# Attention on one core: GpSimd casts tied to VectorE's PSUM reads, and eight score groups on VectorE

## The chip, the core and the metric

The kernel runs on one core of a Trainium2 chip. The time is the device time of one execution in microseconds, the median of ten runs: 122.35 us (121.79 to 123.35). A core has a matrix engine (TensorE, PE in the profile, with PEld for its weight loads), VectorE (DVE), ScalarE (ACT), GpSimd (POOL) and SyncE (SP), whose queue issues nearly all transfers here. SBUF is the on-chip memory; PSUM is the small memory that TensorE writes its results to. Each engine works through its own instructions in order; semaphores hold an instruction until what it needs is done.

## The reference

```python
# q, k, v: (8 batches, 8 heads, 512 positions, 64) float32
scale = 1.0 / np.sqrt(64)
scores = np.einsum('bhqd,bhkd->bhqk', q, k) * scale
scores = scores - scores.max(axis=-1, keepdims=True)
attn = np.exp(scores)
attn = attn / attn.sum(axis=-1, keepdims=True)
out = np.einsum('bhqk,bhkd->bhqd', attn, v)
```

The kernel leaves out the subtraction of the maximum, which cancels in the quotient, and gets the sum from a column of ones that stands beside v.

## The kernel before, in words

The 64 heads are 32 pairs, g = 0 to 31. For each pair the kernel loads q, k and v (256 KB each, float32), casts them to float16, transposes q and k on TensorE, copies the transposed tile from PSUM to SBUF, and then works through eight blocks of scores: 128 keys by 512 queries for each of four key chunks c and two heads h. Two blocks make a group, numbered m; pair g has groups 4g to 4g + 3, and the last two blocks of all stand alone, so there are 129 groups. Scores of a group fill one tile `st` of 128 x 1024 float32 in PSUM (two banks); there are three such tiles. So the scores of group m can start only when whatever reads group m - 3 is done with it.

Most groups get their exponential on ScalarE (L391). Some get it on VectorE instead, in six instructions: `raise_` (L406) reads the scores from PSUM and writes z to SBUF, which frees the PSUM tile. Five `pass_` instructions follow, from SBUF to SBUF: the first takes the mantissa bits (m, L420), and four make a quartic polynomial of it (y, y, y and the result `pd`, L430). The float16 result is the upper half of each 32-bit word. In the names of this text, pass 86.3 is pass 3 (counted from 0) of group 86, and raise 102 the raise of group 102.

TensorE then multiplies the exponentials by v (`values`, L464): a unit is 128 queries of one head, four matmuls of 65 columns. Seven units share a PSUM bank; `normalise` (a reciprocal, L442, and a multiplication, L443) empties the bank on VectorE, and each head that is complete is stored from there (L451). "Norm 168" is the one that begins with unit 168. Two PSUM banks are shared between these outputs and the transposes, which `copy` (L364) empties on VectorE. "Copy 26" is that of pair 26. The last head of all (L479) is summed over the key chunks as they come, and is normalised and stored apart (L491 to L499).

The order is not left to a scheduler: the block at the end of the kernel is written with manual order, and `Plan` makes the list of steps. It holds a clock for TensorE, ScalarE and VectorE with assumed durations (`COPY`, `NORM`, `RAISE`, `PASSES`), and picks the next step of each engine from what would be ready. `for_dve` decides whether a group goes to VectorE: only when no pass of another group is waiting (`AHEAD` 0), at most `MOST` groups, none in the last `LAST_PAIRS` pairs. `LATE_NORM` and `LATE_COPY` say how late a copy or norm may be made by starting a pass before it, `MARGIN` stretches the passes, `SLACK` is added before values may use what VectorE made. On the chip only the resulting order counts; the assumed times are not used.

GpSimd does the casts (L340 for q and k, L332 for v) in the order of `feed(g)`, which comes at the first group of pair g: it issues the loads of pair g + 5, then the casts of q and k of pair g + 3, then of v of pair g + 2. A cast waits for its load and for a free buffer, and for nothing else.

Of the kernel before, what the change touches and what calls it, by code (L numbers as in the profile page):

```python
# [9 lines left out]
FP16 = mybir.dt.float16  # L10
# [3 lines left out]
AluOp = mybir.AluOpType  # L14


class Plan:
# [17 lines left out]

    COPY, NORM, RAISE = (615, 700), (307, 390), (1145, 1225)
    NORM_COLUMN, PASS_DONE = 67, 80
    PASSES = (690, 1335, 1335, 1335, 1335)
    FIRST_EXP = 5260
    STEP = 5  # L40
    FIRST_UNIT = 4

    LATE_NORM, LATE_COPY, HURRY, SOON, BACKLOG = 600, 800, 1000, 220, 1000
    LAST_PAIRS, AHEAD, MARGIN, SLACK, MOST = 5, 0, 1.1, 0, 7

    def __init__(self, groups, pairs, first):
        self.groups, self.pairs = groups, pairs
# [151 lines left out]
    def step_dve(self, t):  # L199
        now = [x for x in self.ready if x[0] <= t]  # L200
        if now:
# [11 lines left out]
            else:  # L213
                self.dve = t + self.RAISE[0]
                self.read[what[0]] = t + self.RAISE[1] + self.TO_PE
                self.passes += [(what[0], s) for s in range(len(self.PASSES))]
        elif self.passes:
            m, s = self.passes[0]
            end = t + int(self.MARGIN * self.PASSES[s])
            late = {"copy": self.LATE_COPY, "norm": self.LATE_NORM, "raise": self.LATE_NORM}  # L220
            if all(x[0] > end - late[x[1]] for x in self.ready):
                self.passes.pop(0)
                self.note(t, "pass", m, s)
                self.dve = end
                if s == len(self.PASSES) - 1:
                    self.exps[m] = end + self.PASS_DONE + self.TO_PE + self.SLACK
# [15 lines left out]
def kernel(  # L242
# [30 lines left out]
    qpool = ctx.enter_context(tc.tile_pool(name="qk16", bufs=3))  # L273
# [17 lines left out]
    raw = {}  # L291
    qkp = {}
    tqk = {}
    tps = {}
# [34 lines left out]
    def cast_v(g):  # L329
        if g >= NP:  # L330
            return
        nc.gpsimd.tensor_copy(out=vps[g % NV][:, :, :, 0:D], in_=raw[g]["v"][:, :, :, :])  # L332

    def cast_qk(g):
        if g >= NP:
            return
        t = qpool.tile([P, 2, NI, P], FP16, tag="qkp", name=f"qkp_{g}")
        for n, name in ((1, "k"), (0, "q")):
            eng = nc.vector if (g, name) == (1, "q") else nc.gpsimd
            eng.tensor_copy(  # L340
                out=t[:, n].rearrange("p i (h d) -> p h i d", h=2),
                in_=raw[g][name][:, :, :, :],
            )
        qkp[g] = t

    def feed(g):
        load(g + 5, "kqv")
        cast_qk(g + 3)
        cast_v(g + 2)

    def transposes(g, n, bank):
        if n == 0:
            tqk[g] = tpool.tile([P, 2, S], FP16, tag="tqk", name=f"tqk_{g}")
            tps[g] = ps_x.tile([P, 2, NI, P], FP16, tag=f"x{bank}", name=f"tp_{g}")
        n = 1 - n
        for i in range(NI):
            nc.tensor.transpose(tps[g][:, n, i, :], qkp[g][:, n, i, :], ident)  # L357

    def copy(g):
        if g == 1:  # L360
            for n in (1, 0):
                nc.vector.tensor_copy(out=tqk[g][:, n], in_=tps[g][:, n].rearrange("p i c -> p (i c)"))  # L362
            return
        nc.vector.tensor_copy(  # L364
            out=tqk[g][:, :, :], in_=tps.pop(g).rearrange("p n i c -> p n (i c)")
        )

    def scores(m, on_dve):
# [32 lines left out]
    QUARTIC = (0.013185735294320473 * 2.0**-78, 0.1618325836988675 * 2.0**-26, -0.6832878102805021, 0.5087543266551143 * 2.0**26)  # L401

    def raise_(m):
        r = raised[m]
        r["z"] = wpool.tile([P, 2, S], U32, tag="z", name=f"z_{m}")
        nc.vector.tensor_scalar(  # L406
            out=r["z"][:, :, :],
            in0=r["st"][:, :, :],
            scalar1=scale * 1.4426950408889634 * 2.0**26,
            scalar2=15 * 2.0**26,  # L410
            op0=AluOp.mult,
            op1=AluOp.add,
        )

    def pass_(m, s):
        r = raised[m]
        if s == 0:
            r["m"] = wpool.tile([P, 2, S], U32, tag="m", name=f"m_{m}")
            r["y"] = wpool.tile([P, 2, S], FP32, tag="y", name=f"y_{m}")
            nc.vector.tensor_scalar(  # L420
                out=r["m"][:, :, :],
                in0=r["z"][:, :, :],
                scalar1=0x03FFFFFF,
                scalar2=0x04000000,
                op0=AluOp.bitwise_and,
                op1=AluOp.bitwise_or,
            )
            return
        n = s - 1
        nc.vector.scalar_tensor_tensor(  # L430
            out=r["bits"][:, :, :] if n == 3 else r["y"][:, :, :],
            in0=r["m"][:, :, :] if n == 0 else r["y"][:, :, :],
            scalar=QUARTIC[n],
            in1=r["z"][:, :, :] if n == 3 else r["m"][:, :, :],
            op0=AluOp.mult if n == 0 else AluOp.add,
            op1=AluOp.add if n == 3 else AluOp.mult,
        )

    def normalise(u, n):
        o, x = os[u // 7], u % 7  # L440
        rc = opool.tile([P, 7, 1], FP32, tag="rc", name=f"rc_{u}")
        nc.vector.reciprocal(out=rc[:, 0:n], in_=o[:, x : x + n, D : D + 1])  # L442
        nc.vector.tensor_tensor(  # L443
            out=ring[:, u % NU : u % NU + n, :],
            in0=o[:, x : x + n, 0:D],
            in1=rc[:, 0:n].broadcast_to([P, n, D]),
            op=AluOp.mult,
        )
        while heads and heads[0][2] + NI <= u + n:
            g, h, u0 = heads.pop(0)  # L450
            nc.sync.dma_start(  # L451
                out=source(out, g)[:, h], in_=ring[:, u0 % NU : u0 % NU + NI, :]
            )

    def values(g, h, y, u, bank):

        if (g, h) == (LAST, 1):
            return last_values(y, bank)
        if y == 0:
            heads.append((g, h, u))  # L460
        if u // 7 not in os:
            os[u // 7] = ps_x.tile([P, 7, D + 1], FP32, tag=f"x{bank}", name=f"o_{u // 7}")
        for c in range(NI):
            nc.tensor.matmul(  # L464
                os[u // 7][:, u % 7, :],
                blocks[(g, c, h)][:, y * P : (y + 1) * P],
                vps[g % NV][:, h, c, :],
                start=(c == 0),
                stop=(c == NI - 1),
            )  # L470
# [132 lines left out]
    with tc.manual_schedule():  # L603
        first_loads()
        load(1, "kq")
        load(0, "v")
        for g in range(2, 5):
            load(g, "kq")
            load(g - 1, "v")
        load(4, "v")  # L610
        make_identity(nc, ident)
        for n in range(NV):
            nc.vector.memset(vps[n][:, :, :, D : D + 1], 1.0)
        first_pair()
        cast_qk(1)
        cast_v(0)
        cast_qk(2)
        cast_v(1)
        feed(0)
        do = {  # L620
            "transposes": transposes,
            "scores": scores,
            "values": values,
            "feed": feed,
            "raise": raise_,
            "copy": lambda g, b: copy(g),
            "pass": pass_,
            "norm": lambda u, n, b: normalise(u, n),
        }
        for what, *args in Plan(groups, NP, 3).run():  # L630
            do[what](*args)
# [30 lines left out]
```

## Time and profile before

| What | Value |
|---|---|
| Median of ten runs | 122.35 us |
| The profiled execution | 122.26 us |
| Its span, first to last instruction | 120.5 us |
| ScalarE busy | 113.5 us, 94% |
| TensorE busy | 104.3 us, 87% |
| VectorE busy | 99.5 us, 83% |
| GpSimd busy | 77.9 us, 65% |
| Moved by DMA | 33.82 MB |
| Granted TensorE clock, mean | 0.992 |

In the lists of groups, a row gives line, engine, operation, what is written from what, shapes and count, then after the bar the busy time in us, the mean of one in ns, and the idle time of that engine just before such instructions. In a timeline, a row gives the start and duration in us, engine, line, operation, tiles and count, and in brackets the idle time before it and what ended that. Records of ScalarE and VectorE can overlap their successor's, so the step from one start to the next is shorter than the duration.

### The profile page before, as it was taken

Reading aid. Unit: us, or ns where it says so; the run is one execution under the profiler, and the core shown is the slowest. Engines: PE = TensorE matmul, PEld = TensorE weight load, DVE = VectorE, ACT = ScalarE, POOL = GpSimd, SP = SyncE. Lnnn points to the kernel's source line nnn. Section 1 sums busy time; section 2 is a strip of 40 time slices with the busy share of each in tenths; the row PEclk is TensorE's granted clock in tenths of the full one; section 3 lists DMA queues with packets and bytes.
Section 4 is the critical chain, followed back from the end, with each engine's and each line's share of the span. In section 5 each row is a group of like instructions: output and inputs, shape, how many; then the busy total and the mean of one; then the engine's idle time right before and its main releaser. Section 6 shows DMA issues by size and latency. Waiting matters only on the chain.

```text
span 120.5 us, 3950 instructions
## 1 busy us (share of the span) xinstructions
PE 104.3 (87%) x1557; PEld 66.2 (55%) x1557; DVE 99.5 (83%) x171; ACT 113.5 (94%) x126; POOL 77.9 (65%) x101
## 2 busy tenths in 40 slices
PE   7977988899897989889987998999988889989970
PEld 2543645466463766457653656656754556667550
DVE  1457997999999998988999988898979999986261
ACT  4599999999999999999999999999999999999970
POOL 2469999995887476945886985775869499100000
PEclk9999999999999999999999999999999999999996
DMA  3999999999999999999999899999999981414253
GB/s 101 297 372 382 384 377 385 381 349 298 348 354 304 272 294 347 312 316 277 305 340 300 271 273 320 339 277 348 336 327 313 331 278 50 132 48 133 93 169 95
DMA packets 35603, 33.82 MB, mean 281 GB/s; under 512 B 2688, under 2 KB 35584, under 8 KB 35584
## 3 DMA queue, kind: packets, MB, share of 16 engines
q1 hardware_dynamic: 35152, 33.24, 85.4%
q10 hardware_dynamic: 432, 0.33, 0.8%
q8 instruction: 12, 0.20, 0.7%
q14 instruction: 7, 0.06, 0.1%
HBM read 25.17 MB, written 8.39 MB: 278 GB/s over the span
## 4 chain that ended last, share of the span: by engine, by line
ACT 50%; PE 27%; DVE 10%; issue 7%; DMA 2%; SPq 1%; ACTq 0%
ACT pt L391 50%; PE st L386 11%; PE o L464 8%; PE tp L357 3%; PE st_0a L512 3%; DVE ring L443 3%; DMA k<-in_k_dram 2%; DVE z L406 2%; DVE tqk L364 1%; DVE pd L430 1%; DVE rc L442 1%; PE st L555 1%; SPq L451 1%; DVE tqk L362 1%; DVE m L420 0%
## 5 line engine op out<-in xcount | busy, mean ns | idle before, releaser
L391 ACT ACTIVATE pt<-st 128x1024 f16<-128x1024 f32 (+1 forms) x119 | 108.5, 1291 | 0.1
L386 PE MATMUL st<-tqk 64*128 64x512 f16 x248 | 46.1, 382 | 10.8 <-ACT pt L391 7.4
L464 PEld LDWEIGHTS <-pt 128*128 128x128 f16 x952 | 35.6, 98 | 11.2 <-issue 9.1
L464 PE MATMUL o<-vp,pt 128*128 128x65 f16 x952 | 41.6, 194 | 0.2
L340 POOL CAST qkp<-k 128x512 f16<-128x512 f32 x31 | 28.6, 922 | 19.1 <-DMA k<-in_k_dram 6.9
L332 POOL CAST vp<-v 128x512 f16<-128x512 f32 x32 | 28.6, 894 | 1.2 <-DMA v<-in_v_dram 1.0
L386 PEld LDWEIGHTS <-tqk 64*128 64x128 f16 x248 | 13.5, 93 | 27.7 <-issue 18.8
L443 DVE TENSOR_TENSOR ring<-o,rc 128x448 f32<-128x448 f32 (+2 forms) x37 | 22.7, 612 | 1.3
L340 POOL CAST qkp<-q 128x512 f16<-128x512 f32 x30 | 22.3, 745 | 1.6 <-DMA q<-in_q_dram 1.5
L364 DVE COPY tqk<-tp 128x1024 f16<-128x1024 f16 x30 | 20.5, 686 | 2.6 <-PE tp L357 2.1
L357 PE MATMUL tp<-ident,qkp 128*128 128x128 f16 x248 | 19.2, 220 | 0.4 <-DVE ring L443 0.4
L430 DVE SCALAR_TENSOR_TENSOR y<-y,m 128x1024 f32<-128x1024 f32 x14 | 18.7, 1336 | 0.0
L357 PEld LDWEIGHTS <-qkp 128*128 128x128 f16 x248 | 14.1, 98 | 7.4 <-issue 4.3
L442 DVE RECIPROCAL rc<-o 128x7 f32<-128x7 f32 (+2 forms) x37 | 7.4, 199 | 7.2 <-PE o L464 7.0
L430 DVE SCALAR_TENSOR_TENSOR pd<-y,z 128x1024 uint32<-128x1024 f32 x7 | 9.6, 1373 | 0.0
L406 DVE TENSOR_SCALAR z<-st 128x1024 uint32<-128x1024 f32 x7 | 8.5, 1219 | 1.2 <-PE st L386 1.2
L430 DVE SCALAR_TENSOR_TENSOR y<-m 128x1024 f32<-128x1024 uint32 x7 | 8.9, 1278 | 0.0
L464 PE MATMUL o<-vp,pd 128*128 128x65 f16 x56 | 8.2, 194 | 0.0
L464 PEld LDWEIGHTS <-pd 128*128 128x128 f16 x56 | 5.5, 98 | 0.0
L420 DVE TENSOR_SCALAR m<-z 128x1024 uint32<-128x1024 uint32 x7 | 5.2, 737 | 0.0
L512 PE MATMUL st_0a<-const-bfloat16-1.0 128*128 128x512 bf16 (+1 forms) x11 | 3.5, 484 | 0.8 <-PEq L646 0.8
L512 PEld LDWEIGHTS <-const-bfloat16-1.0 128*128 128x128 bf16 x15 | 1.7, 131 | 2.4 <-issue 2.4
(44 smaller groups left out, 19.7 us busy)
## 6 DMA issues: line engine op xcount, KB each, us to landing
out_dram<-ring SPq DMA_DIRECT2D x63, 128.0 KB, 3.8
k<-in_k_dram SPq DMA_DIRECT2D x31, 256.0 KB, 4.7
q<-in_q_dram SPq DMA_DIRECT2D x31, 256.0 KB, 4.9
v<-in_v_dram SPq DMA_DIRECT2D x27, 256.0 KB, 5.1
v<-in_v_dram SPq DMA_DIRECT2D x10, 128.0 KB, 4.9
k<-in_k_dram ACTq DMA_DIRECT2D x2, 128.0 KB, 2.8
q<-in_q_dram SPq DMA_DIRECT2D x2, 128.0 KB, 2.6
out_dram<-obl SPq DMA_DIRECT2D x1, 64.0 KB, 1.6
```

What stands on the lines that cost most here:

```text
L332: nc.gpsimd.tensor_copy(out=vps[g % NV][:, :, :, 0:D], in_=raw[g]["v"][:, :, :, :])
L340: eng.tensor_copy(out=t[:, n].rearrange("p i (h d) -> p h i d", h=2), in_=raw[g][name][:, :, :, :],)
L357: nc.tensor.transpose(tps[g][:, n, i, :], qkp[g][:, n, i, :], ident)
L364: nc.vector.tensor_copy(out=tqk[g][:, :, :], in_=tps.pop(g).rearrange("p n i c -> p n (i c)"))
L386: nc.tensor.matmul(st[:, x, :], kc, qc, start=True, stop=True)
L391: nc.scalar.activation(out=pt[:, 0:size, :], in_=st[:, 0:size, :], func=EXP, scale=scale)
L406: nc.vector.tensor_scalar(out=r["z"][:, :, :], in0=r["st"][:, :, :], scalar1=scale * 1.4426950408889634 * 2.0**26, scalar2=15 * 2.0**26, o ...
L430: nc.vector.scalar_tensor_tensor(out=r["bits"][:, :, :] if n == 3 else r["y"][:, :, :], in0=r["m"][:, :, :] if n == 0 else r["y"][:, :, :] ...
L442: nc.vector.reciprocal(out=rc[:, 0:n], in_=o[:, x : x + n, D : D + 1])
L443: nc.vector.tensor_tensor(out=ring[:, u % NU : u % NU + n, :], in0=o[:, x : x + n, 0:D], in1=rc[:, 0:n].broadcast_to([P, n, D]), op=AluOp. ...
L464: nc.tensor.matmul(os[u // 7][:, u % 7, :], blocks[(g, c, h)][:, y * P : (y + 1) * P], vps[g % NV][:, h, c, :], start=(c == 0), stop=(c == ...
L512: nc.tensor.matmul(dst[:, 0:n], ones[:, 0:P], ones[:, 0:n], start=True, stop=True)
```

## The change

There are two parts. First, `feed` no longer issues casts but puts them in a list (`hold`). `copy`, `raise_` and `normalise`, the three steps that read PSUM on VectorE, each take one cast from the list (a raise two) and issue it with a dependency on the VectorE instruction recorded last, that is the one before the PSUM read. If the list has more than six entries, the oldest are issued without such a dependency; `needed` does the same when transposes or values come up whose cast is still in the list. In the order that results, 78 casts are released by VectorE's steps, 10 leave because the list is too long, and none leave by `needed`.

Second, the constants of `Plan` change, and with them the order. Eight groups go to VectorE instead of seven: 6, 17, 32, 46, 60, 72, 86 and 102, where it was 6, 22, 37, 53, 69, 86 and 102. The places of copies, norms, passes and values move with that.

```diff
-    PASSES = (690, 1335, 1335, 1335, 1335)
+    PASSES = (660, 1200, 1200, 1200, 1200)
...
-    LATE_NORM, LATE_COPY, HURRY, SOON, BACKLOG = 600, 800, 1000, 220, 1000
-    LAST_PAIRS, AHEAD, MARGIN, SLACK, MOST = 5, 0, 1.1, 0, 7
+    LATE_NORM, LATE_COPY, HURRY, SOON, BACKLOG = 1300, 1400, 1100, 220, 1000
+    LAST_PAIRS, AHEAD, MARGIN, SLACK, MOST = 3, 0, 1.05, 400, 8
...
+    def dve(ins):
+        latest[:] = [ins]
+        return ins
+
+    def release(n=1):
+        for g, name in held[:n]:
+            ins = cast(g, name)
+            if latest:
[...]
+        del held[:n]
+
+    def hold(g, names):
+        held.extend((g, name) for name in names if g < NP)
+        while len(held) > 6:
+            cast(*held.pop(0))
+
+    def needed(g, names):
+        while any((g, name) in held for name in names):
+            cast(*held.pop(0))
 
     def feed(g):
         load(g + 5, "kqv")
-        cast_qk(g + 3)
-        cast_v(g + 2)
+        hold(g + 3, "kq")
+        hold(g + 2, "v")
 
     def transposes(g, n, bank):
         if n == 0:
+            needed(g, "kq")
...
     def copy(g):
...
-        nc.vector.tensor_copy(
-            out=tqk[g][:, :, :], in_=tps.pop(g).rearrange("p n i c -> p n (i c)")
+        release()
+        dve(
+            nc.vector.tensor_copy(
+                out=tqk[g][:, :, :], in_=tps.pop(g).rearrange("p n i c -> p n (i c)")
+            )
         )
...
     def raise_(m):
+        release(2)
...
     def normalise(u, n):
         o, x = os[u // 7], u % 7
         rc = opool.tile([P, 7, 1], FP32, tag="rc", name=f"rc_{u}")
+        release()
...
         if y == 0:
+            needed(g, "v")
             heads.append((g, h, u))
```

`cast(g, name)` is `cast_qk` and `cast_v` in one, for one tensor at a time, and `dve(...)` stands around the copies, raises, passes and the multiplication of `normalise`.

More of the change, by code (lines that the diff above doesn't have):

```diff
@@ L327, in load, with cast @@
             nc.sync.dma_start(out=t[:, :, :, :], in_=source(src, g))
-    def cast_v(g):
+    def cast(g, name):
         if g >= NP:
             return
[L332 to L342, printed above, removed]
-            )
-        qkp[g] = t
+        if name == "v":
+            return nc.gpsimd.tensor_copy(
+                out=vps[g % NV][:, :, :, 0:D], in_=raw[g]["v"][:, :, :, :]
+            )
+        if g not in qkp:
+            qkp[g] = qpool.tile([P, 2, NI, P], FP16, tag="qkp", name=f"qkp_{g}")
+        eng = nc.vector if (g, name) == (1, "q") else nc.gpsimd
+        return eng.tensor_copy(
+            out=qkp[g][:, "qk".index(name)].rearrange("p i (h d) -> p h i d", h=2),
+            in_=raw[g][name][:, :, :, :],
+        )
+    held = []
+    latest = []
+    SYNC = mybir.DependencyInfo(mybir.DependencyClass.Sync, mybir.DependencyReason.DATA)
+    def dve(ins):
[5 more added lines that the diff above has]
+            if latest:
+                tc.add_manual_dep(ins.ins, latest[0].ins.name, SYNC, reason="SBUF ports")
+        del held[:n]
[6 more added lines that the diff above has]
+            cast(*held.pop(0))
     def feed(g):
         load(g + 5, "kqv")
-        cast_qk(g + 3)
-        cast_v(g + 2)
+        hold(g + 3, "kq")
+        hold(g + 2, "v")
     def transposes(g, n, bank):
         if n == 0:
+            needed(g, "kq")
             tqk[g] = tpool.tile([P, 2, S], FP16, tag="tqk", name=f"tqk_{g}")
@@ L361, in copy @@
             for n in (1, 0):
-                nc.vector.tensor_copy(out=tqk[g][:, n], in_=tps[g][:, n].rearrange("p i c -> p (i c)"))
+                dve(nc.vector.tensor_copy(out=tqk[g][:, n], in_=tps[g][:, n].rearrange("p i c -> p (i c)")))
             return
-        nc.vector.tensor_copy(
-            out=tqk[g][:, :, :], in_=tps.pop(g).rearrange("p n i c -> p n (i c)")
+        release()
+        dve(
+            nc.vector.tensor_copy(
+                out=tqk[g][:, :, :], in_=tps.pop(g).rearrange("p n i c -> p n (i c)")
+            )
         )
@@ L403, in raise_ @@
     def raise_(m):
+        release(2)
         r = raised[m]
         r["z"] = wpool.tile([P, 2, S], U32, tag="z", name=f"z_{m}")
[L406 to L412, printed above, removed]
+        dve(
+            nc.vector.tensor_scalar(
+                out=r["z"][:, :, :],
+                in0=r["st"][:, :, :],
+                scalar1=scale * 1.4426950408889634 * 2.0**26,
+                scalar2=15 * 2.0**26,
+                op0=AluOp.mult,
+                op1=AluOp.add,
+            )
         )
@@ L419, in pass_ @@
             r["y"] = wpool.tile([P, 2, S], FP32, tag="y", name=f"y_{m}")
[L420 to L426, printed above, removed]
+            dve(
+                nc.vector.tensor_scalar(
+                    out=r["m"][:, :, :],
+                    in0=r["z"][:, :, :],
+                    scalar1=0x03FFFFFF,
+                    scalar2=0x04000000,
+                    op0=AluOp.bitwise_and,
+                    op1=AluOp.bitwise_or,
+                )
             )
@@ L429, in pass_ @@
         n = s - 1
[L430 to L436, printed above, removed]
+        dve(
+            nc.vector.scalar_tensor_tensor(
+                out=r["bits"][:, :, :] if n == 3 else r["y"][:, :, :],
+                in0=r["m"][:, :, :] if n == 0 else r["y"][:, :, :],
+                scalar=QUARTIC[n],
+                in1=r["z"][:, :, :] if n == 3 else r["m"][:, :, :],
+                op0=AluOp.mult if n == 0 else AluOp.add,
+                op1=AluOp.add if n == 3 else AluOp.mult,
+            )
         )
@@ L441, in normalise @@
         rc = opool.tile([P, 7, 1], FP32, tag="rc", name=f"rc_{u}")
+        release()
         nc.vector.reciprocal(out=rc[:, 0:n], in_=o[:, x : x + n, D : D + 1])
[L443 to L447, printed above, removed]
+        dve(
+            nc.vector.tensor_tensor(
+                out=ring[:, u % NU : u % NU + n, :],
+                in0=o[:, x : x + n, 0:D],
+                in1=rc[:, 0:n].broadcast_to([P, n, D]),
+                op=AluOp.mult,
+            )
         )
@@ L614 @@
         first_pair()
[L615 to L618, printed above, removed]
+        for g, names in ((1, "kq"), (0, "v"), (2, "kq"), (1, "v")):
+            for name in names:
+                cast(g, name)
         feed(0)
```

## The prediction, made before the changed kernel had run

> **What bounds the kernel now.** I read the page's first part, then the timeline of ScalarE, to see whether its busy time is really without a hole.
>
> ```profile
> PE 104.3 (87%) x1557; PEld 66.2 (55%) x1557; DVE 99.5 (83%) x171; ACT 113.5 (94%) x126; POOL 77.9 (65%) x101
> ...
> L391 ACT ACTIVATE pt<-st 128x1024 f16<-128x1024 f32 (+1 forms) x119 | 108.5, 1291 | 0.1
> ```
> ```profile
> 8.24 108.53 ACT L391 ACTIVATE pt<-st 128x1024 f16<-128x1024 f32 x119
> ```
>
> ScalarE runs 119 exponentials in one unbroken stretch of 108.53 us, with 0.1 us of idle time. The last two are half size (0.49 us each by the single records' ends), so a full one costs (108.53 - 0.98) / 117 = 0.919; the single records end 0.917 apart from the second of the stretch on. The mean of 1291 ns is not the cost: consecutive records overlap. So ScalarE sets the end, and one exponential less is worth 0.917 us as long as it never runs dry. Its margin is small: three score tiles in PSUM allow TensorE to be only so far ahead. I take an exponential that starts late to last 1.02 us (the first full ones, L562, took 1.03), so scores that end later than 0.14 us before the previous exponential's end cost time. By the records the scores beat that limit by at most 1.25 us, and by 0.33 or less around the groups that VectorE computes, since one of the three tiles is then with VectorE.
>
> Next is VectorE. From its first raise to the last pass (9.76 to 107.22 us), cut at the raises:
>
> ```profile
> core 0: us, DVE busy (x), PEclk, DMA share, GB/s
> ...
> sum 97.46, DVE 90.11; mean DVE 12.87
> ```
>
> It has 7.35 us of idle time for 7 groups. What the casts cost it is seen in the timelines of VectorE and GpSimd:
>
> ```profile
> 77.50 0.69 DVE L364 COPY tqk<-tp 128x1024 f16<-128x1024 f16 x1
> 78.11 1.47 DVE L430 SCALAR_TENSOR_TENSOR pd<-y,z 128x1024 uint32<-128x1024 f32 x1
> ...
> 104.74 1.22 DVE L430 SCALAR_TENSOR_TENSOR y<-y,m 128x1024 f32<-128x1024 f32 x1
> ```
> ```profile
> 77.89 0.62 POOL L340 CAST qkp<-k 128x512 f16<-128x512 f32 x1 [0.89 <-PE st L386]
> 78.47 1.59 POOL L340 CAST qkp<-q 128x512 f16<-128x512 f32 x1
> ```
>
> A cast beside a PSUM copy takes 0.62 and leaves the copy alone. A pass that begins during a cast is held until it ends (1.47 against the undisturbed 1.22), and a cast that begins during a pass waits for the pass (1.59). So only a cast that is still running when a pass starts costs VectorE anything.
>
> **The change part by part.** *One exponential leaves ScalarE* (8 groups on VectorE instead of 7, scores 6, 17, 32, 46, 60, 72, 86, 102): -0.92.
>
> *VectorE gets one group more:* raise, m and four passes. By the starts of successive instructions at best 1.13 + 0.60 + 4 x 1.13 = 6.25 us (raise to the following copy 1.13, pass to the next instruction 1.13). [...] The rows show the next one starting 0.08 before the record's end (77.50 + 0.69 against 78.11), so I take 6.25.
>
> *The held casts give VectorE time back.* The 28 large passes sum to 37.25; 28 at the shortest (1.207) make 33.8, so 3.45 is excess, and 0.38 for m: at most 3.8. The order of the changed program has 88 held casts: 78 are issued at a copy, norm or raise, each waiting for the VectorE instruction before it, and 10 leave unheld because the list is full. A released cast does not begin with the copy: the previous record ends 0.08 after the copy began, and GpSimd started 0.12 to 0.13 after the TensorE work it had waited for. So it runs from about 0.20 to 0.78 of a copy that hands over at 0.61. In the rows a cast that overhung a pass by 0.21 cost it 0.07, one by 0.11 nothing. I estimate 0.05 per pass after a copy, and a recovery of about 3 of the 3.8 (ends: nothing, and all). VectorE's idle time becomes 7.35 - 0.92 - 6.25 + 3 = 3.2 us; without recovery 0.2[...].
>
> *Later casts.* Before, q's cast ended 5 to 9 us ahead of its transposes for most pairs from 9 on; now it waits for a later VectorE job. Tightest are pairs 5, 27 and 30, whose q is released by the last job that the order has ahead of their transposes (norm 7, raise 102, norm 196): a cast ends 0.78 after such a job starts, so TensorE may wait there for about half a copy, 0.3 us. Behind it on TensorE stand scores, but with 0.3 to 1.25 in hand: I take 0.05 in all. Loads and stores keep their order on SP; the release of an input buffer still comes before the load that needs it, so no load waits. DMA cost: nothing, covered by the five pairs of prefetch; if that went, a load takes 4.7 us to land.
>
> *The order around group 102.* This is where I see a loss. Before, copy 26 (L364) came ahead of raise 102:
>
> ```profile
> 91.45 0.68 DVE L364 COPY tqk<-tp 128x1024 f16<-128x1024 f16 x1
> 92.00 0.39 PE L386 MATMUL st<-tqk 64*128 64x512 f16 x2 [0.52 <-ACT pt L391]
> 92.05 1.58 DVE L430 SCALAR_TENSOR_TENSOR pd<-y,z 128x1024 uint32<-128x1024 f32 x1
> ...
> 93.56 1.21 DVE L406 TENSOR_SCALAR z<-st 128x1024 uint32<-128x1024 f32 x1
> 93.83 0.39 PE L386 MATMUL st<-tqk 64*128 64x512 f16 x2
> ```
>
> Scores 102 ended at 92.39, raise 102 was 1.16 late, and scores 104 (pair 26) still ended at 94.23, 0.33 ahead of need. In the changed order VectorE does pass 86.3, norm 168, pass 86.4, norm 175, raise 102, and only then copy 26, which scores 104 read. On before's clock: copy 25 not before 87.6 (its transposes end 87.44), then 0.61 + 0.77 + 1.13 + 0.77 + 1.13 + 0.77 (copy, norm, pass, norm, pass, norm) puts raise 102 at 92.8; plus 1.13 and 0.69, copy 26 ends 94.6; scores take 0.06 + 0.41, to 95.1. The limit is 94.23 + 0.33 = 94.56. Loss 0.55, with 0.05 per pass 0.65: I take 0.60. Ends: 0.15 if raise 102 starts at once, 1.3 if it is as late as before. Elsewhere the copy of the next pair comes ahead of the raise, or the pair is two or more groups off, so I find no second such place.
>
> *The tail.* In the changed order 14 units of values follow the last scores, against 8. Before:
>
> ```profile
> 114.74 0.60 PE L386 MATMUL st<-tqk 64*128 64x512 f16 x2
> 115.27 0.68 PE L464 MATMUL o<-vp,pt 128*128 128x65 f16 x16
> 115.86 0.77 PE L479 MATMUL o_last<-vp,pt 128*128 128x65 f16 x12
> 116.82 0.30 PE L479 MATMUL o_last<-vp,pt 128*128 128x65 f16 x4 [0.20 <-ACT pt L391]
> ```
>
> A unit takes about 0.15 (four in 0.68 with the fill). With ScalarE's end as X (116.77 before), the last unit ended at X + 0.36. Now: last scores near X - 1.6, six units to X - 0.7, norm 245 (0.88) frees the bank that the last head needs near X + 0.2, its four units with the fill to X + 0.92. Loss 0.55; 0.2 if the bank is no obstacle, 0.75 if the last scores are no earlier than now. The norm of the last 4 whole units (0.58) fits meanwhile.
>
> Sum: -0.92 + 0.60 + 0.55 + 0.05 = +0.28. The profiled run took 122.26 (span 120.5, 1.76 around it): 122.54; the median lies 0.09 above it: **122.6**.
>
> **The rivals.** *The gain comes through* (121.6): raise 102 finds VectorE free (0.15) and the tail costs 0.2: -0.92 + 0.35 = -0.57, or less where TensorE gets rid of its units early. For it: 7.35 us of idle time that already exists. Against: both losses lie in a fixed order. *VectorE becomes the bound* (124.2): its idle time came from waits for TensorE (L442 alone 7.0 us for L464), and such waits do not vanish. If the casts overhang the passes as now, half of the 3.8 comes back and 2.1 is left; if it needs 4, ScalarE waits the other 1.9: 122.35 + 1.9. It decides once raises are later than about 1.4 us behind their scores (1.16 late was still hidden). *The casts do not move off the passes*: recovery nil, seen in passes still near 1.33; at 0.2 us of idle left that ends as the second.
>
> **How the numbers follow.** Offsetting gain and losses 0.45, gain 0.20, VectorE bound 0.35 (with casts that stay in the passes). A measurement here can tell about 0.5% (0.6 us) from no change. Of the first case, own range 121.9 to 123.3, some lies above 122.96, so: faster 0.20, same 0.41, slower 0.39. The range runs from the gain (121.6) to VectorE bound (124.2).
>
> **What would show it.** 118 exponentials at 0.917; a ScalarE gap of about 0.6 ahead of pair 26's scores with copy 26 behind raise 102; passes at 1.21 to 1.28, casts mostly 0.62; the last values 0.9 after the last exponential. Wrong if passes stay at 1.33, if gaps appear at several raises, or if no gap appears and the span drops by 0.9.

## The result, and the profile after

The changed kernel took 124.76 us (median of 14 runs, 122.91 to 126.60) against 122.40 (49 runs, 121.78 to 124.50). The ratio of the comparison is 1.0129, 95% interval 1.0099 to 1.0159: slower by 1.3%, some 123.9 us on the median of before. The ratio leaves out the seven slowest runs of the changed kernel; over all runs the medians are 1.9% apart. Its runs lie far apart because TensorE was granted half its clock for a stretch in 11 of the 14 (mean clock 0.964 to 0.980, against 0.993 or 0.994), and the profiled run (125.47, span 123.7) is one with two such stretches. Of 84 runs of the kernel before whose clock is on record, one lies at 0.98, the others at 0.989 or more.

The page's busy times and ScalarE's group, after:

```profile
PE 104.9 (85%) x1557; PEld 66.2 (53%) x1557; DVE 104.3 (84%) x177; ACT 113.2 (92%) x125; POOL 65.5 (53%) x101
...
L419 ACT ACTIVATE pt<-st 128x1024 f16<-128x1024 f32 (+1 forms) x118 | 108.2, 1127 | 2.9 <-PE st L414 2.6
```

There is one exponential fewer, as meant, but ScalarE now waits for scores (2.9 us where it was 0.1). By the ends of the single records ScalarE ended at 119.20 where it was 116.77: 0.92 less for the exponential, 3.35 more in gaps. From there to the end of the span it took 4.49 instead of 3.72. Together that is the 3.2 us between the spans.

The gaps in ScalarE's timeline are two near 20 us, one near 74 and one near 97 (each line has its start, its busy time, the engine and the work; in brackets stand the idle time and what ended it; the loss is about 0.1 more than the idle time, since an exponential that starts late lasted 1.02 us, as in the first row, where the step is 0.917):

```profile
19.82 1.02 ACT L419 ACTIVATE pt<-st 128x1024 f16<-128x1024 f32 x1 [0.43 <-PE st L414]
...
21.78 3.08 ACT L419 ACTIVATE pt<-st 128x1024 f16<-128x1024 f32 x3 [0.94 <-PE st L414]
```
```profile
74.44 1.94 ACT L419 ACTIVATE pt<-st 128x1024 f16<-128x1024 f32 x2 [0.81 <-PE st L414]
```
```profile
95.80 1.28 DVE L391 COPY tqk<-tp 128x1024 f16<-128x1024 f16 x2
...
96.53 0.82 PE L414 MATMUL st<-tqk 64*128 64x512 f16 x6 [0.65 <-DVE tqk L391]
...
97.03 2.86 ACT L419 ACTIVATE pt<-st 128x1024 f16<-128x1024 f32 x3 [0.47 <-PE st L414]
```

The last one is the gap that was forecast: scores 104 wait for copy 26. It cost 0.58 us; scores 16, 18 and 19 cost 0.53, 1.04 and 0.23, scores 76 and 78 0.14 and 0.92.

TensorE in stretches of 1 us around the first gaps (busy time and instructions, granted clock, DMA share, GB/s):

```profile
16.00:17.00 1.00, 0.87 (x12) 1.00 1.05 363
17.00:18.00 1.00, 0.09 (x2) 1.00 1.09 377
18.00:19.00 1.00, 0.56 (x7) 1.00 1.08 381
19.00:20.00 1.00, 1.00 (x12) 0.59 1.10 385
20.00:21.00 1.00, 1.00 (x17) 0.50 1.09 384
21.00:22.00 1.00, 1.00 (x11) 0.50 1.10 383
22.00:23.00 1.00, 1.00 (x16) 0.71 1.09 382
```

TensorE stands nearly idle from 17 to 18 us, and shortly after its clock is at one half: by the shares in the fourth and the last row, from 19.18 to 22.59. A second such stretch, 70.38 to 73.79, lies ahead of the gaps at scores 76 and 78. What TensorE waits for near 17 us is in the timeline of all engines:

```profile
14.61 2.78 DVE L464 SCALAR_TENSOR_TENSOR y<-y,m 128x1024 f32<-128x1024 f32 x2
...
17.31 0.68 DVE L391 COPY tqk<-tp 128x1024 f16<-128x1024 f16 x1
17.61 0.62 POOL L339 CAST qkp<-k 128x512 f16<-128x512 f32 x1 [1.29 <-DVE y L464]
...
18.17 0.62 POOL L339 CAST qkp<-q 128x512 f16<-128x512 f32 x1
18.28 0.40 PE L382 MATMUL tp<-ident,qkp 128*128 128x128 f16 x4 [1.20 <-POOL qkp L339]
...
18.84 0.40 PE L382 MATMUL tp<-ident,qkp 128*128 128x128 f16 x4 [0.16 <-POOL qkp L339]
...
19.17 0.61 PE L414 MATMUL st<-tqk 64*128 64x512 f16 x2
```

Passes 6.2 and 6.3 run in a row, then copy 4, which releases the cast of k of pair 5; norm 7 releases q. The transposes of pair 5 wait for both casts, and scores 16 stand behind these transposes on TensorE.

The tail, on TensorE and VectorE:

```profile
117.66 1.46 PE L503 MATMUL o<-vp,pt 128*128 128x65 f16 x40
...
118.88 0.63 DVE L480 TENSOR_TENSOR ring<-o,rc 128x448 f32<-128x448 f32 x1
...
119.65 0.65 PE L518 MATMUL o_last<-vp,pt 128*128 128x65 f16 x16 [0.54 <-DVE rc L478]
```

Ten whole units follow the last scores (four before), and the last head waits for the bank that norm 245 frees (its multiplication, the second row, ends at 119.51). The last head's last unit ends 1.11 us after ScalarE instead of 0.35.

VectorE's passes did get shorter. By group, after:

```profile
L464 DVE SCALAR_TENSOR_TENSOR y<-y,m 128x1024 f32<-128x1024 f32 x16 | 20.2, 1265 | 0.1
...
L464 DVE SCALAR_TENSOR_TENSOR pd<-y,z 128x1024 uint32<-128x1024 f32 x8 | 10.6, 1320 | 0.1
L464 DVE SCALAR_TENSOR_TENSOR y<-m 128x1024 f32<-128x1024 uint32 x8 | 10.1, 1261 | 0.2
...
L452 DVE TENSOR_SCALAR m<-z 128x1024 uint32<-128x1024 uint32 x8 | 6.4, 796 | 0.0
```

The 32 large passes are 2.3 us above 32 of the shortest of before (0.07 each), where 28 had been 3.45 (0.12 each).

### The profile page after: what moved, and what is told of

It is laid out like the page before. It is cut to its first block, busy times and chain, and to the rows that moved or that the text cites. A ratio compares the mean times of both kernels' runs of the same rounds, so it can differ in the third digit from the quotient of the medians.

```text
span 123.7 us, 4009 instructions
## 1 busy us (share of the span) xinstructions
PE 104.9 (85%) x1557; PEld 66.2 (53%) x1557; DVE 104.3 (84%) x177; ACT 113.2 (92%) x125; POOL 65.5 (53%) x101
## 4 chain that ended last, share of the span: by engine, by line
PE 34%; DVE 30%; ACT 16%; issue 8%; DMA 7%; POOL 1%; SPq 1%; ACTq 0%
ACT pt L419 16%; PE o L503 12%; PE st L414 11%; DVE y L464 10%; DVE tqk L391 6%; PE tp L382 5%; DMA v<-in_v_dram 5%; DVE ring L480 5%; DVE z L436 3%; PE st_0a L551 3%; DMA q<-in_q_dram 2%; DVE m L452 2%; DVE rc L478 2%; POOL qkp L339 1%; DVE pd L464 1%
## 5 line engine op out<-in xcount | busy, mean ns | idle before, releaser
L503 PEld LDWEIGHTS <-pt 128*128 128x128 f16 x944 | 37.3, 100 | 11.5 <-issue 9.5
L339 POOL CAST qkp<-k 128x512 f16<-128x512 f32 x31 | 19.4, 626 | 22.4 <-DVE rc L478 6.9
L414 PEld LDWEIGHTS <-tqk 64*128 64x128 f16 x248 | 11.8, 94 | 24.7 <-issue 16.9
L339 POOL CAST qkp<-q 128x512 f16<-128x512 f32 x30 | 18.5, 616 | 9.2 <-DVE y L464 5.7
L382 PE MATMUL tp<-ident,qkp 128*128 128x128 f16 x248 | 20.7, 223 | 3.1 <-POOL qkp L339 1.5
L464 DVE SCALAR_TENSOR_TENSOR y<-y,m 128x1024 f32<-128x1024 f32 x16 | 20.2, 1265 | 0.1
L436 DVE TENSOR_SCALAR z<-st 128x1024 uint32<-128x1024 f32 x8 | 9.8, 1220 | 2.4 <-PE st L414 2.4
L464 DVE SCALAR_TENSOR_TENSOR y<-m 128x1024 f32<-128x1024 uint32 x8 | 10.1, 1261 | 0.2
L503 PE MATMUL o<-vp,pd 128*128 128x65 f16 x64 | 9.5, 195 | 0.0
L452 DVE TENSOR_SCALAR m<-z 128x1024 uint32<-128x1024 uint32 x8 | 6.4, 796 | 0.0
```

Of the source, the lines that this page charges most:

```text
L339: return eng.tensor_copy(out=qkp[g][:, "qk".index(name)].rearrange("p i (h d) -> p h i d", h=2), in_=raw[g][name][:, :, :, :],)
L414: nc.tensor.matmul(st[:, x, :], kc, qc, start=True, stop=True)
L436: nc.vector.tensor_scalar(out=r["z"][:, :, :], in0=r["st"][:, :, :], scalar1=scale * 1.4426950408889634 * 2.0**26, scalar2=15 * 2.0**26, o ...
L464: nc.vector.scalar_tensor_tensor(out=r["bits"][:, :, :] if n == 3 else r["y"][:, :, :], in0=r["m"][:, :, :] if n == 0 else r["y"][:, :, :] ...
L503: nc.tensor.matmul(os[u // 7][:, u % 7, :], blocks[(g, c, h)][:, y * P : (y + 1) * P], vps[g % NV][:, h, c, :], start=(c == 0), stop=(c == ...
```

## The experiments

I started from theory A: the losses are the place of copy 26, the tail, and casts that reach TensorE late. The rivals were B, that VectorE cannot carry eight groups, and C, that holding the casts is the whole loss.

### One part alone: the new order without held casts

```diff
     def hold(g, names):
-        held.extend((g, name) for name in names if g < NP)
-        while len(held) > 6:
-            cast(*held.pop(0))
+        for name in names:
+            cast(g, name)
```

> The new order with eight groups, but every cast issued at its feed as before. Theory A (the held casts leave TensorE waiting early on, its clock halves there, and the rest of the loss is the place of copy 26 and the tail): the wait for the casts of pair 5 is gone, no half clock near 20 us, but the gap before pair 26's scores (0.6) and the late tail (0.7) stay and the passes are back near 1.33: about 123.3 us. Theory B (eight groups are too many for VectorE, held casts or not): no better than the changed kernel, 124.8 to 126, with raises late by over 1.4 us and gaps on ScalarE at several of them. Theory C (holding is the whole loss): 122.0 or less.

Measured: 126.03 us (4 runs, 125.58 to 127.01), ratio 1.0308, 1.0235 to 1.0380. Worse than the changed kernel, against C, and worse than I had put under A. The time is the one that B gave, though no raise was later than 1.02 us. Its passes:

```profile
L463 DVE SCALAR_TENSOR_TENSOR y<-y,m 128x1024 f32<-128x1024 f32 x16 | 22.3, 1394 | 0.1
...
L463 DVE SCALAR_TENSOR_TENSOR pd<-y,z 128x1024 uint32<-128x1024 f32 x8 | 11.8, 1474 | 0.1
L463 DVE SCALAR_TENSOR_TENSOR y<-m 128x1024 f32<-128x1024 uint32 x8 | 10.9, 1364 | 0.2
```

The three groups sum to 45.0 us, 4.1 more than with held casts (40.9), and ScalarE has small gaps in a dozen places instead of a few long ones; the gap before pair 26 is 1.43. So in this order the held casts are not the loss: without them it is over 1 us longer still. TensorE's wait ahead of pair 5's transposes is there too, for copy 4:

```profile
19.27 0.61 PE L381 MATMUL tp<-ident,qkp 128*128 128x128 f16 x8 [1.44 <-DVE tqk L390]
```

### The other part alone: held casts in the old order

The constants of `Plan` as before, all else as changed.

> The casts held, but the constants and so the order of before, seven groups. Theory A: TensorE waits for casts that come late at pairs 4 to 6; where that halves its clock ScalarE runs dry for 1 to 2 us, so 122.5 to 124, spread out like the changed kernel's runs. Theory B: VectorE has its 7.35 us of idle time and 2 to 3 us more, so 122.4, no change. Theory C: as slow as the changed kernel, 124.5.

Measured: 122.43 us (12 runs), ratio 0.9999, 0.9980 to 1.0018. No change, as B had it, and no half clock in any run (mean clock 0.991 or more); A was wrong to expect late casts to matter here. But the passes are no shorter either: 37.2 us for 28, against 37.25 before. In the old order holding costs nothing and wins nothing. The trace shows why: 13 of the 28 passes still last over 1.25 us, each directly behind a copy or a norm during which a cast had begun that ran on into the pass, as here:

```profile
27.34 0.62 POOL L333 CAST vp<-v 128x512 f16<-128x512 f32 x1
27.40 1.62 DVE L464 SCALAR_TENSOR_TENSOR y<-m 128x1024 f32<-128x1024 uint32 x1
```

In the changed kernel's profile only two passes are of this kind.

### Copy 26 ahead of raise 102

```diff
-        for what, *args in Plan(groups, NP, 3).run():
+        steps = Plan(groups, NP, 3).run()
+        for g, m in ((26, 102),):
+            step = next(s for s in steps if s[:2] == ("copy", g))
+            steps.remove(step)
+            steps.insert(steps.index(("raise", m)), step)
+        for what, *args in steps:
```

> The changed kernel with one step moved: copy 26 stands before raise 102 instead of behind it. Theory A: ScalarE's gap of 0.58 us before pair 26 is gone, all else stays: 0.5 to 0.6 below the changed kernel, 124.2. Theory B: raise 102 is then 0.6 later, and the gap moves to scores 105: no change, 124.8. Theory C: no change.

Measured: 125.08 us (9 runs, 122.91 to 125.67), ratio 1.0065, 1.0031 to 1.0100. The nine runs fall into two sets: three at a mean clock of 0.993 to 0.995 took 122.91 to 123.26, six at 0.964 to 0.980 took 124.89 to 125.67. The changed kernel's runs at full clock took 122.91, 123.79 and 123.99. The profile says it more plainly than the medians: VectorE does copy 26 and then the raise, and ScalarE runs through.

```profile
90.13 6.90 ACT L419 ACTIVATE pt<-st 128x1024 f16<-128x1024 f32 x7
...
92.39 0.68 DVE L391 COPY tqk<-tp 128x1024 f16<-128x1024 f16 x1
...
92.99 1.22 DVE L436 TENSOR_SCALAR z<-st 128x1024 uint32<-128x1024 f32 x1
```

The gap of 0.58 is gone, and did not move to scores 105. A later one of 0.41, before pair 29, is new. The mechanism of the forecast holds. The scatter is now the larger matter.

### The first casts free

```diff
     def hold(g, names):
+        if g < 6:
+            while held:
+                cast(*held.pop(0))
+            for name in names:
+                cast(g, name)
+            return
         held.extend((g, name) for name in names if g < NP)
```

> The changed kernel, but the casts up to pair 6 are issued at once; from there on they are held as in the change. Theory A: TensorE no longer waits 1.2 us for pair 5's casts, its clock stays full near 20 us in every run, ScalarE's gaps at scores 16 to 19 (1.8 us together) vanish: the mean granted clock loses one of its two drops, and the median falls by 0.8 to 1.8 us, to 123 to 124. Theory B: the gaps come back one pair later, 124.8. Theory C: in between, about 124.5.

Measured: 123.44 us (4 runs, 123.29 to 124.17), ratio 1.0103, 1.0057 to 1.0150. Two of four runs kept the full clock (1.000 against 0.981 and 0.982). The profiled one did not, and has the gaps at 16, 18 and 19 as before (0.59, 1.04, 0.18). Freeing these casts alone does not take the first gap away: the transposes of pair 5 now wait for copy 4 instead (1.32 us), which frees their PSUM bank.

### Copies 3 and 4 ahead of passes

```diff
+        for step, g in ((("pass", 6, 1), 3), (("pass", 6, 3), 4)):
+            steps.remove(step)
+            at = next(n for n, s in enumerate(steps) if s[:2] == ("copy", g))
+            steps.insert(at + 1, step)
```

> The changed kernel with two passes of group 6 moved: 6.1 behind copy 3 and 6.3 behind copy 4, so copy 4 no longer waits for pass 6.3. Theory D (the loss at 16 to 24 us is copy 4, late behind two passes in a row: it holds the transposes of pair 5 and with them scores 16, TensorE idles 1.2 to 1.7 us, and in many runs its clock then halves): copy 4 at about 16.0 instead of 17.3, no gap at scores 16 to 19, no half clock near 20 us, median 0.8 to 2 us below the changed kernel: 122.9 to 123.9, with the gap before pair 26 and the tail left. Theory E (the held casts make the wait): the transposes of pair 5 still wait for their casts, 124.5 or more.

Measured: 124.52 us (4 runs, 123.09 to 125.76), ratio 1.0124, 1.0046 to 1.0202. That the place of these two copies makes the first gap was wrong: copy 4 is early (16.2), and scores 16 are as late as ever. The cast of q now hangs behind norm 7, which hangs behind pass 6.3, and TensorE waits 1.36 us for it. Two waits cover each other here.

### Both moves

This kernel has the edits of the two runs on copies, with casts held as in the change.

> Both moves together: copy 26 before raise 102, and two passes of group 6 behind copies 3 and 4. Theory D: no gap longer than 0.4 anywhere, clock full, ScalarE's end 0.9 before that of the kernel before, and the tail still 0.76 longer: 122.4 to 122.8. If other places take the gain: 123.5 or more.

Measured: 125.98 us (4 runs, 123.14 to 126.36), three of them at a clock of 0.964 to 0.967, so one run is left to compare (123.14), too few for a ratio. Expected under D was 122.4 to 122.8. The gap before pair 26 is gone in its profile, those at 16 to 20 are there.

### Dummy matmuls where TensorE is idle

```diff
             needed(g, "kq")
+            if g == 5:
+                early[16] = ps_st.tile([P, 2, S], FP32, tag="st", name="st_16")
+                for _ in range(3):
+                    busy(early[16][:, 0], S)
...
-        st = ps_st.tile([P, 2, S], FP32, tag="st", name=f"st_{m}")
+        st = early.pop(m) if m in early else ps_st.tile([P, 2, S], FP32, tag="st", name=f"st_{m}")
```

> The changed kernel with three dummy matmuls of 512 columns ahead of the transposes of pair 5, where TensorE is idle (into the score tile that is written next). Theory D with the clock as the larger part: copy 4 and scores 16 stay late (gap of about 0.5 before scores 16), but the clock stays full near 20 us more often, and scores 18 and 19 are in time: median about 123.5. If the clock does not follow TensorE's idle time: half clock as often as in the changed kernel, and 124.8 or a little more.

Measured: 123.58 us (9 runs, 123.11 to 125.20), ratio 1.0099, 1.0064 to 1.0134. The order is that of the changed kernel; three useless matmuls were added, 0.81 us in the profile, which themselves wait for the score tile they write. One run of nine lost the clock (0.978, the others 0.992 or more), where it was 11 of 14, and the median is 1.2 us lower. In the profile the gap before scores 16 stands (0.66), the one before 18 is 0.24 instead of 1.04, and the one before 19 is gone.

```profile
18.06 0.81 PE L556 MATMUL st<-const-bfloat16-1.0 128*128 128x512 bf16 x3 [0.52 <-ACT pt L424]
...
19.08 0.40 PE L387 MATMUL tp<-ident,qkp 128*128 128x128 f16 x4 [0.21 <-POOL qkp L339]
...
20.91 0.61 PE L419 MATMUL st<-tqk 64*128 64x512 f16 x4
```

Four score matmuls take 0.61 here and 1.04 in the changed kernel at the same place:

```profile
20.70 1.04 PE L414 MATMUL st<-tqk 64*128 64x512 f16 x4
```

That the useless matmuls keep the clock rests on the count of runs; one profile at full clock does not show it, since other profiles without them kept it too (copy 26 first is one). So where a stretch at half clock follows, the late casts and copies cost twice: once as a wait of 0.5 to 0.7, and once more in that stretch (0.50 granted from 19.18 to 22.59 in the changed kernel's profile).

### Both covers removed

Three edits at once: the first casts free, passes 6.1 and 6.3 behind copies 3 and 4, copy 26 ahead of raise 102.

> Three edits at once: casts up to pair 6 issued at once, two passes of group 6 behind copies 3 and 4, copy 26 before raise 102. Theory F (two covers: the transposes of pair 5 wait for copy 4 and for the casts held behind pass 6.3, and both end at the same time, so removing one alone did nothing): with both removed the gaps at scores 16 to 19 are gone, the clock stays full near 20 us, and what is left is the tail (0.76) and the gap of 0.4 before pair 29: 122.4 to 122.9. If a third cause stands behind these two, the gap before scores 16 stays near 0.6 and the median at 123.5 or more.

Measured: 125.02 us (4 runs, 124.15 to 125.75), ratio 1.0196, 1.0135 to 1.0257, all runs below a clock of 0.982. That two covers are all there is was wrong too: there is a third.

```profile
17.21 1.58 DVE L470 SCALAR_TENSOR_TENSOR y<-y,m 128x1024 f32<-128x1024 f32 x1
...
17.67 1.60 POOL L339 CAST qkp<-q 128x512 f16<-128x512 f32 x1
...
19.33 0.61 PE L388 MATMUL tp<-ident,qkp 128*128 128x128 f16 x4 [1.15 <-POOL qkp L339]
```

The cast of q of pair 5 is held by nobody, but pass 6.3 has begun, so it takes 1.60 instead of 0.61 or 0.62 and ends at 19.27. With so few copies and norms between the passes of group 6, GpSimd gets its casts through late whether they are held (18.79 in the changed kernel, 19.06 with copies 3 and 4 ahead of passes) or not.

### Scores 16 ahead of the transposes of pair 5

```diff
+        late = [s for s in steps if s[:2] == ("transposes", 5)]
+        steps = [s for s in steps if s not in late]
+        at = next(n for n, s in enumerate(steps) if s[:2] == ("scores", 16))
+        steps[at + 1 : at + 1] = late
```

> The changed kernel with one move on TensorE alone: scores 16 stand before the transposes of pair 5 instead of behind them (as in the order before the change). Theory G (GpSimd cannot get q5 cast before 18.8 to 19.3 us in this order, whether held or not, because passes of group 6 shut it out; the loss comes only from scores 16 queueing behind the transposes that wait for it): scores 16 end near 18.4, the gaps at scores 16 and 18 (0.53 and 1.04) are gone or under 0.3, and fewer runs lose the clock near 20 us: median 123.0 to 123.9. If the wait only moves on: the gap stands at scores 18 or 20 with the same length, 124.8.

Measured: 123.79 us (4 runs, 122.84 to 125.44), ratio 1.0107, 1.0046 to 1.0168. The gap before scores 16 is gone (they end at 18.33), 0.47 is left before 18 and 0.14 before 20; those before 18 and 19 had been 1.27. But TensorE still idles 1.31 us ahead of scores 16, now for copy 4, and two runs of four lost the clock (0.965 and 0.980, the others 0.990 and 0.995).

```profile
17.94 0.39 PE L414 MATMUL st<-tqk 64*128 64x512 f16 x2 [1.31 <-DVE tqk L391]
```

So the place of scores 16 behind the transposes is what makes the gap before 16; the idle time has a cause of its own, the two passes ahead of copy 4.

### Eight groups in other orders

If the order is at fault and not the number of groups, another order must do better. First, the planner's constants set so that no copy stands behind two passes and copy 26 is ahead of raise 102:

```diff
-    PASSES = (660, 1200, 1200, 1200, 1200)
+    PASSES = (680, 1180, 1180, 1180, 1180)
...
-    LATE_NORM, LATE_COPY, HURRY, SOON, BACKLOG = 1300, 1400, 1100, 220, 1000
-    LAST_PAIRS, AHEAD, MARGIN, SLACK, MOST = 3, 0, 1.05, 400, 8
+    LATE_NORM, LATE_COPY, HURRY, SOON, BACKLOG = 600, 800, 800, 300, 900
+    LAST_PAIRS, AHEAD, MARGIN, SLACK, MOST = 5, 0, 1.0, 400, 8
```

> Eight groups and held casts with other constants of the planner (lateness limits 600 and 800 as before, passes 1180 without a stretch): no copy behind two passes, copy 26 before raise 102, and 8 units after the last scores instead of 14. Theory D (the order, not the eighth group and not the held casts): ScalarE without gaps and the tail as before: 0.9 less than before, 121.5; up to 122 if one gap remains. Theory B (eight groups are too many for VectorE even with held casts): 123 or more, raises over 1.4 us late.

Measured: 123.00 us (20 runs, 122.68 to 123.93), ratio 1.0047, 1.0025 to 1.0069. No run lost the clock (0.990 or more), and the tail is back at 0.35 with 8 units behind the last scores. But ScalarE has a gap at every other group of VectorE:

```profile
26.47 23.94 ACT L419 ACTIVATE pt<-st 128x1024 f16<-128x1024 f32 x26 [0.49 <-PE st L414]
50.59 23.98 ACT L419 ACTIVATE pt<-st 128x1024 f16<-128x1024 f32 x26 [0.18 <-PE st L414]
74.79 23.97 ACT L419 ACTIVATE pt<-st 128x1024 f16<-128x1024 f32 x26 [0.23 <-PE st L414]
98.99 18.50 ACT L419 ACTIVATE pt<-st 128x1024 f16<-128x1024 f32 x21 [0.23 <-PE st L414]
```

Raises 18, 46, 74 and 102 come 1.2 to 1.4 us after their scores. This is the rival in which VectorE becomes the bound, and not the 121.5 that I had put under D: the plan took the passes at 1180 ns, and they measured 1.36 us, with VectorE busy for 7.93 of the 8 us from 18 to 26. So a second order, planned near the measured durations:

```diff
-    COPY, NORM, RAISE = (615, 700), (307, 390), (1145, 1225)
+    COPY, NORM, RAISE = (630, 715), (307, 390), (1145, 1225)
...
-    PASSES = (660, 1200, 1200, 1200, 1200)
+    PASSES = (680, 1290, 1290, 1290, 1290)
...
-    LATE_NORM, LATE_COPY, HURRY, SOON, BACKLOG = 1300, 1400, 1100, 220, 1000
-    LAST_PAIRS, AHEAD, MARGIN, SLACK, MOST = 3, 0, 1.05, 400, 8
+    LATE_NORM, LATE_COPY, HURRY, SOON, BACKLOG = 1000, 800, 800, 220, 800
+    LAST_PAIRS, AHEAD, MARGIN, SLACK, MOST = 2, 0, 1.0, 200, 8
```

> Eight groups, held casts, and planner constants close to what was measured (passes 1290 without a stretch, copies 630, lateness limits 1000 and 800, last group 109): raises at most 0.5 us behind their scores in the plan, no copy behind two passes at the start, 8 units after the last scores. If eight groups can pay at all: 121.5 to 122.0, tail 0.35. If VectorE is the bound for eight groups in any order: gaps at several raises, 122.5 or more, as in the gentler order.

Measured: 122.22 us (10 runs, 121.28 to 122.65) against 122.59 before: ratio 0.9967, 0.9936 to 0.9998. That lies between the two cases put before. From 26 us on ScalarE runs 99 exponentials without a gap of note:

```profile
15.64 10.19 ACT L419 ACTIVATE pt<-st 128x1024 f16<-128x1024 f32 x11 [0.22 <-PE st L414]
26.07 90.12 ACT L419 ACTIVATE pt<-st 128x1024 f16<-128x1024 f32 x99 [0.23 <-PE st L414]
```

ScalarE ends at 116.19 (116.77 before; its first exponentials came 0.4 earlier too), the tail is 0.35. And the same order with the casts up to pair 6 free:

> The same order, with the casts up to pair 6 issued at once. If held casts keep TensorE waiting at the start: 0.3 to 0.6 below the run with all casts held; otherwise the same or 0.2 longer, because the passes of group 6 are held up by casts again.

Measured: 122.21 us (20 runs, 121.44 to 123.55), ratio 0.9961, 0.9936 to 0.9986. No different from the former: holding the first casts costs nothing in an order that leaves room for them. With held casts, eight groups are here faster than seven by 0.3 to 0.4%; these are the only two kernels whose interval lies below 1, the first of them barely. Whether this order needs held casts is not shown: it was not run without them. Raise 18 is still 1.42 us late in both, and gaps before 27.5 us cost 0.8 and 1.2 us in the two profiles.

## Why the prediction was right or wrong, point by point

The two forecast losses were there, and the time by the comparison's ratio (123.9) lies inside the range, while the median over all runs (124.76) lies above it. The likeliest case, an offset of gain and losses at 122.6, did not come: the kernel was slower by 1.3%. That its time lies inside the range at all is luck. The upper part of the range was made for VectorE as the bound, which did not happen; what filled it was a wait of TensorE that the sum had at 0.05, and a clock that it did not have. With the clock left aside the terms close: -0.92 + 0.58 + 0.76 + 1.03 = 1.45 us (the 1.03 are the gaps at scores 16 and 18 in the profile of copy 26 first, at full clock), and the changed kernel's three runs at full clock have a median 1.39 above 122.40.

*One exponential, 0.917:* right. There are 118, and the step between undisturbed ends is unchanged.

*The order around group 102, 0.60:* right. It was 0.58 in the profile, raise 102 was 0.33 late (0.4 by the working), and moving copy 26 alone removed the gap.

*The tail, 0.55:* mechanism right, the term was undersized: about 0.76, in every profile with 14 units behind the last scores (1.10 to 1.11 after ScalarE), against 0.35 as before in the profiles with 8. I had let the last scores run early, at X - 1.6; the changed kernel's ended at 117.73, X - 1.48. The upper end given, 0.75, was the value.

*Later casts, 0.05:* wrong, and the step that failed: 1.03 us at full clock, 1.81 in the profiled run. It named pair 5 and a wait of TensorE, and then let the wait vanish in the 0.3 to 1.25 us that the scores have in hand. It did not look at what stands behind pair 5's transposes: scores 16, which before the change stood ahead of them. And the wait was not 0.3 but 1.2, because copy 4 and both casts sit behind passes 6.2 and 6.3. Held casts are not even needed for it: without them the same transposes waited 1.44 for copy 4. "I find no second such place" is the same error: I asked where a raise precedes a copy, not where two passes do. The changed order has five such copies, 3, 4, 18, 20 and 29, the order before none.

*The clock:* in no step at all. The profile before shows full clock up to 118.52 us, behind the last matmul (117.12), so nothing in it warned of a price for idle time on TensorE.

In the changed kernel's profile the clock changes at 19.18, 22.59, 70.38, 73.79 and 121.58 us; each stretch at half clock within the work lasts 3.41 us, and all five times lie whole multiples of 3.413 us apart (30 of them from the first to the last). TensorE in windows of that length, cut at these times (busy time and instructions, granted clock, DMA share, GB/s):

```profile
15.77:19.18 3.41, 1.93 (x26) 1.00 1.07 374
19.18:22.59 3.41, 3.41 (x38) 0.50 1.09 382
...
66.97:70.38 3.41, 1.96 (x20) 1.00 0.88 281
70.38:73.79 3.41, 3.32 (x38) 0.50 0.73 228
```

The profile of copy 26 first has the same steps and the same wait near 17 us, and kept the clock. Its windows, counted back in steps of 3.413 from its drop behind the work at 120.23, cut that wait in two:

```profile
14.41:17.82 3.41, 2.22 (x24) 1.00 1.09 379
17.82:21.24 3.42, 2.76 (x44) 1.00 1.09 383
```

So in these two profiles the same steps went with half clock behind a window with 1.93 us of busy time, and with full clock behind windows with 2.22 and 2.76. In the fourteen profiles the eight drops within the work follow windows with 1.60 to 1.99 us of busy time, and, after the first 10 us, every window of the work with 2.08 or more was followed by full clock. Busy time is not the whole measure: a window with 1.94 at the start of the run with both moves kept the clock, and one with 2.20 at the very end of the second order did not. That the place of the windows decides is my reading of these profiles, and not shown by a run.

The price: the changed kernel's runs have a median of 123.79 at full clock (3 runs), 124.84 with a mean clock near 0.98 (9), and 126.04 near 0.964 (2), about 1.1 us for each drop. The gaps at scores 76 and 78 (1.06 together) are the second drop's: a gap at scores 78 stands in each of the three profiles with such a drop (0.91 to 1.11) and in none of the six others with these constants, and four score matmuls that last 1.04 at 70.98 last 0.60 in the profile with the first casts free, which has the same steps there.

*VectorE's ledger, 3 of 3.8 us back:* too high against the kernel before. By the working's own yardstick (1.207 for a pass, 0.68 for m) the excess was 3.45 + 0.38 = 3.8 us for seven groups and is 2.3 + 0.9 = 3.2 for eight, where 3 us back would have left 0.8. Against the same order without held casts the passes won 4.1 us, so holding returned mostly what the new order had cost. About 0.6 of the excess lies in passes 6.1 and 6.3 (1.50 and 1.52), ahead of copy 4. In the old order the passes won nothing, which I did not foresee.

*The rivals.* That VectorE becomes the bound was not what happened: raises were at most 0.85 late, under the 1.4 from which it was to decide, and another order carries eight groups. In the gentler order, with every other raise 1.2 to 1.4 late, it did. That the gain comes through needs an order that neither kernel of the comparison has.

Not settled: where the runs without a profile lost the clock, since only their mean clock is on record; whether the work in such a window decides, and how much of it is enough to keep the clock; and what the second order would take without held casts.

## What to carry to other kernels

With orders written out by hand, a term costed at "hidden" must be followed to the instruction that stands behind the waiting one on its engine; three covers lay over one another here, and removing one or two of them changed little. Work that is moved to a nearly full engine pays by its order: eight groups gave 1.0129 with copies behind two passes, 1.0047 with passes planned shorter than they ran, and 0.9967 with neither (other constants of the plan differed too). And a wait on TensorE can come with a cost beyond its length: behind the one of 1.20 us near 17 us the granted clock was 0.50 for 3.41 us, and the runs' medians put about 1.1 us on each such drop. Look at the granted clock of the stretch behind a wait.

## What was not expected of the hardware

Half a clock for 3.41 us after a stretch of the same length in which TensorE was busy for little more than half the time (1.93 of 3.41 us); some such stretch came, by the mean clock, in 11 of 14 runs, and in 1 of 9 with 0.81 us of dummy matmuls put ahead of it. And a cast that waits through one pass gets in before a second pass that follows directly: the second then lasts 1.51 to 1.52 us instead of 1.21, in four places of the changed kernel's profile. In that profile two passes in a row were dearer for it.
